# DeltaNet stage of a hybrid layer: scan, inverse, solve and pair preparation in a fixed program order on VectorE and ScalarE, with preparation in pieces two pairs ahead

## The chip, the cores and the metric

The kernel runs as one program on one core of a Trainium2 chip. The time is device time in microseconds, the median of several executions. Engines are named as in the profile: PE is TensorE's matmul, PEld its weight load, DVE is VectorE, ACT is ScalarE, POOL is GpSimd, SP is SyncE, which issues the DMA loads. Each engine takes its instructions in the order in which the program holds them.

## The reference

One layer over 512 latent tokens and 256 context tokens, width 1024, float32. Its token mixing joins softmax attention with a bidirectional gated DeltaNet of 8 heads of 128; the DeltaNet is the part that matters here:

```
# S_t = a_t (I - beta_t k_t k_t^T) S_{t-1} + beta_t k_t v_t^T,  o_t = S_t^T q_t, in chunks
gam = cumsum(log_a)                         # within the chunk
dec = exp(gam_c - gam_s) for c >= s, else 0
a_mat = strict_lower(beta * dec * (k k^T)) + I
u, w = triangular_solve(a_mat, [beta * v, beta * exp(gam) * k])
k_dec, g_last = k * exp(gam_last - gam), exp(gam_last)
q_dec, p = q * exp(gam), dec * (q k^T)
# scan over chunks: v' = u - w S;  o = q_dec S + p v';  S = g_last S + k_dec^T v'
```

It runs once in each direction, over the context first and then over the latent tokens. Chunks are 128 tokens in the kernel, so 6 of them to a head (2 of context, 4 latent).

## The kernel before

The layer is one long stream of projections (128x512 matmuls of split float32 operands, three for each product: high by high, low by high, high by low). The DeltaNet stage lies between 353 and 842 us of the span. Its 8 heads go in 4 pairs, p = 0 to 3, and each pair passes through five parts:

- `gdn_prep(p)` loads kT, and for each of the two heads (hh) and two directions (d) a broadcast of the cumulative decay `gamdr`, into NN and Gb (128x768). A mask is added (`NN<-NN,cst`, `Gb<-Gb,cst`), ACT takes six exponentials, and the two are summed (`NN<-NN,Gb`). It also makes the small tile g and its transpose gT.
- `gdn_solve` multiplies NN by the products k k^T (`pk`, on PE), lays the diagonal 32x32 blocks out as C, transposes to X, scales by gT, and inverts by a loop of 31 steps, each a `prod<-X,R` and an `R<-R,prod`. Then R is scaled by gT and transposed in 32x32 blocks into o_tr and o_nt. The loop is on DVE for pair 0 and on POOL for the others (SPOOL = '123').
- `gdn_inv(p)` builds the whole inverse (TTm) from the blocks, in four groups of products on PE that start with `pb<-o_tr,NN` and `pb<-o_nt,NN`.
- `gdn_scan(p)` runs six steps in both directions: `pb<-S,kT`, the residual r on DVE, `pb<-r,TTm`, then dk (ACT) and dl (DVE), the state S, the output oacc. Decay masks M2 (called M in the profile) come from `decay_mask`, one for each of four latent chunks; the last two steps add `pb<-dl,M` into oacc.
- `gdn_out(p)` normalises oacc, transposes it on PE, multiplies by the gate sz, and splits it into the high and low operands (g_s, g_n, g_k, g_m) of the last DeltaNet projection.

PE's order in this stage is pinned to the order of the program. Around the DeltaNet parts `weave` puts steps of `filler`, the layer's other projections, at set rates; a step of filler is three matmuls. `wait(n)` is n steps of filler alone: WK of them go before the first solve, W0 between the first solve and the first inverse, W1 after each scan. In the stage of pair p, `gdn_inv(p)` is interleaved with the solve of pair p+1, and then comes the scan of pair p beside the output of pair p-1. DVE's and ACT's order there is set by a scheduler, with priorities that the code gives (`early`, `sooner`, `solver`, `first`). Elementwise operations go through small helpers (`tt`, `ts`, `stt`, `act`), so most of DVE's and ACT's rows carry the lines of those: L108, L112 and L114, L117, L120.

Of the kernel before, what the change touches and what calls it, by code (L numbers as in the profile page):

```python
# [6 lines left out]
F32 = mybir.dt.float32  # L7
# [7 lines left out]
P = 128  # L15
D = 1024
# [14 lines left out]
POPS = (1, 3, 5, 7)  # L31
CHUNK, WK, W0, W1, RI, RS, RO = 1, 24, 66, 0, 3.0, 2.8, 2.0
RI0 = 2.4
# [45 lines left out]
def hybrid_layer_body(tc, x, ctxt, xT, consts, cols, rows, w_mod1, w_mod2, w_db, w_aq, w_cm, w_pa, w_pd, w_out,  # L79
# [23 lines left out]
    def dump(name, ap):  # L103
        if dbg is not None and name in dbg:
            SP.dma_start(dbg[name], ap)

    def tt(out, a, b, op, eng=None):
        (eng or V).tensor_tensor(out=out, in0=a, in1=b, op=op)  # L108

    def ts(out, a, s1, op0, s2=None, op1=None, eng=None):  # L110
        if op1 is None:
            (eng or V).tensor_scalar(out=out, in0=a, scalar1=s1, scalar2=None, op0=op0)  # L112
        else:
            (eng or V).tensor_scalar(out=out, in0=a, scalar1=s1, scalar2=s2, op0=op0, op1=op1)  # L114

    def stt(out, a, s, b, op0, op1):
        V.scalar_tensor_tensor(out=out, in0=a, scalar=s, in1=b, op0=op0, op1=op1)  # L117

    def act(out, a, f=AF.Copy, **kw):
        A.activation(out, a, f, **kw)  # L120

# [12 lines left out]
    with es:  # L134
# [738 lines left out]

        def gdn_prep(p, eng=G):
            kT = gq.tile([P, 2, NA], F32, name="kT", tag="kT", bufs=2)
            for hh in range(2):
                SP.dma_start(kT[:, hh, :], kTd[2 * p + hh])
            g = gq.tile([P, 32], F32, name="g", tag="g", bufs=2)
            gT = gq.tile([P, 32], F32, name="gT", tag="gT", bufs=2)
            V.memset(g[:, 24:32], 0.0)  # L880
# [6 lines left out]
            V.transpose(gT, g)  # L887
            NN = gq.tile([P, 12, P], F32, name="NN", tag="NN", bufs=2)
            for hh in range(2):
                u = slice(6 * hh, 6 * hh + 6)  # L890
                Gb = gq.tile([P, 6, P], F32, name="Gb", tag="Gb", bufs=1)
                for d, D in ((0, NN[:, u, :]), (1, Gb)):
                    r0 = d * 48 + p * 12 + hh * 6
                    SP.dma_start(D.rearrange("p a b -> p (a b)"),
                                 gamdr[r0:r0 + 6, :].rearrange("a b -> (a b)").partition_broadcast(P))
                    tt(D, D, msk_s[d].unsqueeze(1).to_broadcast([P, 6, P]), ALU.add, eng)
                    for c in range(6):
                        act(D[:, c, :], D[:, c, :], AF.Exp, scale=-1.0, bias=gam[:, r0 + c:r0 + c + 1])
                tt(NN[:, u, :], NN[:, u, :], Gb, ALU.add, eng)
            return [kT, gT, NN]  # L900

        def gdn_solve(pre, eng):
# [11 lines left out]
            with solver():  # L914
                q4 = lambda nm: gq.tile([P, 32, 32], F32, name=nm, tag="q4", bufs=3)
                C = q4("C")
                for b in range(4):
                    sb = slice(32 * b, 32 * b + 32)
                    V.transpose(C[sb, :, 12:24].rearrange("p j u -> p u j"), NN[sb, :, sb])
# [3 lines left out]
                V.transpose(flat(X), flat(C))  # L923
# [4 lines left out]
                if True:  # L928
                    for j in range(31):
                        m, n = 31 - j, j + 1  # L930
                        prod = gq.tile([P, 272], F32, name="prod", tag="prod")
                        pv = prod[:, 0:m * n].rearrange("p (i k) -> p i k", k=n)
                        tt(pv, X[:, j, j + 1:32].unsqueeze(2).to_broadcast([P, m, n]),
                           R[:, j:j + 1, 0:n].to_broadcast([P, m, n]), ALU.mult, eng)
                        tt(R[:, j + 1:32, 0:n], R[:, j + 1:32, 0:n], pv, ALU.add, eng)
                tt(R, R, gT.unsqueeze(2).to_broadcast([P, 32, 32]), ALU.mult)
                o_tr = q4("o_tr")
                V.transpose(o_tr.rearrange("p u s -> p s u"), R)
                o_nt = q4("o_nt")
                V.transpose(o_nt.rearrange("p u s -> p s u"), R.rearrange("p i k -> p k i"))  # L940
            pre += [o_tr, o_nt]

        def gdn_inv(p, pre):
# [13 lines left out]
            with sooner():  # L957
                for i, ((d, a, b), py) in enumerate(zip(AB, pys)):
                    (V.tensor_copy if i % 2 else act)(Y1[q(a)], py[q(a)])
# [9 lines left out]
            with sooner():  # L969
                for (d, e, f), pz in zip(AB, pzs):  # L970
                    (act if e % 2 else V.tensor_copy)(TTm[q(e), d, :, q(f)], pz[q(e)])
                for d in range(2):
                    a, b = TOP[d]
                    V.transpose(Tm[q(b), :, 32 * (a % 2):32 * (a % 2) + 32], TTm[q(a), d, :, q(b)])
            yield WY[1]

            for hh in range(2):
# [5 lines left out]
                with sooner():  # L983
                    for d in range(2):
                        sA, sB = HV[d]
                        (V.tensor_copy if d else act)(Y2[hh][sA], pys[d][sA])
                yield WY[2 + hh]
# [22 lines left out]

        def gdn_scan(p, pre, seqs):
            kT = pre[0]
# [25 lines left out]

            masks = {c: decay_mask(c) for c in (4, 3, 5, 2)}
            PTs = {}  # L1040
            for st in range(6):
                lat = st >= 2
                if st == 2:
                    oacc = gpool[0].tile([P, 2, 4, P], F32, name="oacc", tag="oacc")
# [24 lines left out]
                for d in range(2):  # L1069
# [7 lines left out]
                    if lat:  # L1077
                        dl = gpool[0].tile([P, 2, P], F32, name="dl", tag="dl", bufs=6)
                        V.tensor_copy(dl, pds[d][:, 0:2, :])
                        dls[(d, c)] = dl  # L1080
                    if st < 5:
# [70 lines left out]
        def gsplit(h):  # L1152
            if h % 2 == 0:
# [4 lines left out]
                elif h == 4:  # L1158
                    ts_ = [gq.tile([P, 12, P], F32R, name="g_n", tag="NN", bufs=2),
                           gq.tile([P, 2, NA], F32R, name="g_k", tag="kT", bufs=2)]  # L1160
                else:
                    ts_ = [gq.tile([P, 2, NA], F32R, name="g_k", tag="kT", bufs=2)]
                    ls = [gpool[0].tile([P, 2, 2, P], F32R, name="g_m", tag="M2", bufs=4) for _ in range(2)]
# [15 lines left out]
        def run(g):  # L1179
            for _ in g:  # L1180
                pass

        with early():
            pre = gdn_prep(0, V if P0 else G)
        pas_es, y_es, yt = ExitStack(), ExitStack(), []
# [116 lines left out]
        def stage(p, pre, nxt):  # L1302
            inv = gdn_inv(p, pre)
            if nxt is not None:
                yield from both(inv, gdn_solve(nxt, G if p + 1 in SPOOL else V))
            else:
                yield from inv

        for p in range(NP):
            cur = pre  # L1310
            pre = gdn_prep(p + 1) if p + 1 < NP else None
            g = stage(p, cur, pre)
# [3 lines left out]
            g = gdn_scan(p, cur, gdn_load(p))  # L1316
            out = (None, gdn_out(0), gdn_out(1), gdn_reload())[p]
# [266 lines left out]
```

## Time and profile before

| | |
|---|---|
| median of 3 runs | 1308.92 us (1308.15 to 1310.53) |
| profiled execution | 1304.85 us, its span 1303.1 us |
| PE busy | 1224.8 us, 94% of the span |
| PEld busy | 1024.0 us, 79% |
| DVE busy | 846.9 us, 65% |
| ACT busy | 625.9 us, 48% |
| POOL busy | 308.9 us, 24% |
| DMA | 170.82 MB, mean 131 GB/s |

A row of a timeline gives start, duration, engine, line, operation, and output <- inputs; a bracket at its end gives the time for which its engine had been idle, and what ended that. A row of PE's waits gives who was waited for, the total, how many times, and the longest. A row of a tile gives minimum, median and maximum duration in ns and the first and last start. In the table by stage each row gives the busy time of the engines in that stretch, then the granted TensorE clock (1.00 is full), the share of time in which the DMA engines were busy, and GB/s.

### The profile page before, as it was taken

Reading aid. Unit: us, or ns where it says so; the run is one execution under the profiler, and the core shown is the slowest. Engines: PE = TensorE matmul, PEld = TensorE weight load, DVE = VectorE, ACT = ScalarE, POOL = GpSimd, SP = SyncE. Lnnn points to the kernel's source line nnn. Section 1 sums busy time; section 2 is a strip of 40 time slices with the busy share of each in tenths; the row PEclk is TensorE's granted clock in tenths of the full one; section 3 lists DMA queues with packets and bytes.
Section 4 is the critical chain, followed back from the end, with each engine's and each line's share of the span. In section 5 each row is a group of like instructions: output and inputs, shape, how many; then the busy total and the mean of one; then the engine's idle time right before and its main releaser. Section 6 shows DMA issues by size and latency. Waiting matters only on the chain.

```text
span 1303.1 us, 20844 instructions
## 1 busy us (share of the span) xinstructions
PE 1224.8 (94%) x7835; PEld 1024.0 (79%) x7835; DVE 846.9 (65%) x1625; ACT 625.9 (48%) x1403; POOL 308.9 (24%) x364
## 2 busy tenths in 40 slices
PE   6899999999967999899998999999999999999997
PEld 3487878899856878778787888778988888888886
DVE  5886977777759986675665556555676666653223
ACT  5454656666576665474444443233454444442221
POOL 1753420000133249659546400000000000000000
PEclk9999999999989999999999999999999999999998
DMA  8656731121383342543632654374032323332331
GB/s 318 228 169 200 233 109 65 65 82 57 116 239 104 123 141 93 177 135 106 195 123 97 188 169 147 120 234 155 19 112 97 97 97 97 97 93 89 98 93 66
DMA packets 70790, 170.82 MB, mean 131 GB/s; under 512 B 7872, under 2 KB 18720, under 8 KB 69280
## 3 DMA queue, kind: packets, MB, share of 16 engines
q1 hardware_dynamic: 70688, 169.47, 39.4%
q8 instruction: 62, 1.02, 0.3%
q14 instruction: 40, 0.33, 0.1%
HBM read 144.23 MB, written 25.21 MB: 130 GB/s over the span
## 4 chain that ended last, share of the span: by engine, by line
PE 66%; POOL 11%; DVE 8%; DMA 5%; issue 3%; ACT 3%; SPq 0%; POOLq 0%; DVEq 0%; ACTq 0%
PE mc L87 32%; PE mb L87 17%; POOL R L108 4%; PE pq L87 4%; POOL prod L108 4%; PE pb L87 4%; PE pS L87 3%; PE ab L87 2%; PE ab L91 1%; DMA Gb<-gamdr 1%; DMA M<-gamdr 1%; PE xb L91 1%; DVE wlo L108 1%; PE pk L87 1%; DMA sz<-gdr 1%
## 5 line engine op out<-in xcount | busy, mean ns | idle before, releaser
L108 DVE TENSOR_TENSOR wlo<-wraw,whi 128x1024 fp32r<-128x1024 f32 x152 | 187.5, 1235 | 163.3 <-ACT whi L120 161.1
L120 ACT ACTIVATE whi<-wraw 128x1024 fp32r<-128x1024 f32 x152 | 159.0, 1048 | 207.3 <-PE mc L87 112.0
L87 PE MATMUL mb<-hxH,whi 128*128 128x512 f32 x384 | 163.6, 426 | 3.2 <-DVE R L108 3.0
L87 PE MATMUL mb<-hxL,whi 128*128 128x512 f32 x384 | 153.6, 400 | 0.0
L87 PE MATMUL mb<-hxH,wlo 128*128 128x512 f32 x384 | 153.2, 399 | 0.0
L87 PE MATMUL mc<-h2H,whi 128*128 128x512 f32 (+1 forms) x376 | 142.9, 380 | 0.3 <-ACT whi L120 0.3
L87 PE MATMUL mc<-h2H,wlo 128*128 128x512 f32 (+1 forms) x376 | 142.1, 378 | 0.5 <-DVE wlo L108 0.5
L87 PE MATMUL mc<-h2L,whi 128*128 128x512 f32 (+1 forms) x376 | 140.7, 374 | 0.0
L108 POOL TENSOR_TENSOR rc<-rc,mhalf 128x2 f32<-128x2 f32 x4 | 3.2, 812 | 461.2 <-DVE rc L114 461.2
L87 PEld LDWEIGHTS mb<-hxH,wlo 128*128 128x128 f32 x384 | 73.1, 190 | 18.0
L87 PEld LDWEIGHTS mb<-hxH,whi 128*128 128x128 f32 x384 | 73.9, 192 | 14.8 <-issue 3.2
L87 PEld LDWEIGHTS mc<-h2H,wlo 128*128 128x128 f32 x376 | 70.5, 188 | 15.3 <-DVE wlo L108 1.0
L87 PEld LDWEIGHTS mb<-hxL,whi 128*128 128x128 f32 x384 | 73.7, 192 | 10.1
L87 PEld LDWEIGHTS mc<-h2L,whi 128*128 128x128 f32 x376 | 70.6, 188 | 13.7
L87 PEld LDWEIGHTS mc<-h2H,whi 128*128 128x128 f32 x376 | 70.7, 188 | 12.7 <-ACT whi L120 0.5
L87 PE MATMUL mc<-aH,whi 128*128 128x512 f32 (+1 forms) x198 | 73.4, 371 | 0.6 <-DVE x L117 0.6
L87 PE MATMUL mc<-aH,wlo 128*128 128x512 f32 (+1 forms) x198 | 73.1, 369 | 0.0
L87 PE MATMUL mc<-aL,whi 128*128 128x512 f32 (+1 forms) x198 | 73.1, 369 | 0.0
L117 DVE SCALAR_TENSOR_TENSOR u<-mc,col,u 128x511 f32<-128x511 f32 x88 | 65.4, 747 | 1.4
L108 POOL TENSOR_TENSOR prod<-X,R 128x31 f32<-128x31 f32 (+15 forms) x93 | 53.5, 575 | 22.2 <-DVE X L108 15.3
L108 POOL TENSOR_TENSOR R<-R,prod 128x31 f32<-128x31 f32 (+15 forms) x93 | 57.1, 614 | 6.8
L87 PE MATMUL pq<-whi,hxH 128*128 128x256 f32 x192 | 55.8, 291 | 0.0
(354 smaller groups left out, 3069.8 us busy)
## 6 DMA issues: line engine op xcount, KB each, us to landing
wraw<-in_w_cm_dram SPq DMA_DIRECT2D x48, 512.0 KB, 3.9
wraw<-in_w_up_dram SPq DMA_DIRECT2D x44, 512.0 KB, 3.7
wmd<-in_w_mod_dram SPq DMA_DIRECT2D x64, 256.0 KB, 3.7
wm<-in_w_mod_dram SPq DMA_DIRECT2D x8, 1024.0 KB, 8.9
wraw<-in_w_down_dram SPq DMA_DIRECT2D x16, 512.0 KB, 3.6
wraw<-in_w_aq_dram SPq DMA_DIRECT2D x12, 512.0 KB, 4.9
M<-gamdr SPq DMA_DIRECT2D x64, 64.0 KB, 4.5
wraw<-in_w_pa_dram SPq DMA_DIRECT2D x8, 512.0 KB, 4.0
```

Of the source, the lines that this page charges most:

```text
L87: i = nc.tensor.matmul(*a, **k)
L91: i = nc.tensor.transpose(*a, **k)
L108: (eng or V).tensor_tensor(out=out, in0=a, in1=b, op=op)
L117: V.scalar_tensor_tensor(out=out, in0=a, scalar=s, in1=b, op0=op0, op1=op1)
L120: A.activation(out, a, f, **kw)
```

## The change

1. `kept(g)` runs a generator with a flag set; `ordered` then pins each DVE and ACT instruction that the generator emits behind the instruction that the program emitted last on that engine, filler included. Solve, preparation of pairs 1 to 3, inverse and scan run so. POOL is not pinned.
2. `gdn_prep` becomes a generator that gives way between its loads, each mask addition and the sum. Pair 1's runs among the steps of W0, and pair p+2's beside the scan of pair p. All mask additions and sums are now on DVE; before, those of pairs 1 to 3 were on POOL. Gb has two buffers instead of one, kT three instead of two.
3. The last product of the solve, R by gT, is on POOL for pairs 1 to 3.
4. o_tr and o_nt leave the end of the solve for `end()`. The scan of pair p calls it for pair p+1 in its last step, behind the copy of dl for d = 1. For pair 0 it is called after W0.
5. The decay masks are made one at each of the scan's first four steps, where all four came ahead of the scan.
6. WK goes from 24 to 30, W0 from 66 to 60, W1 from 0 to 2. The two steps of W1 put six filler matmuls between the end of a scan and the next inverse.

```
-CHUNK, WK, W0, W1, RI, RS, RO = 1, 24, 66, 0, 3.0, 2.8, 2.0
+CHUNK, WK, W0, W1, RI, RS, RO = 1, 30, 60, 2, 3.0, 2.8, 2.0
...
+    keep = [False]
+    def ordered(i, eng=None):
+        return tc.keep_in_program_order(i) if keep[0] and eng is not G else i
+    def kept(g):
+        while True:
+            keep[0] = True
+            try:
+                w = next(g)
+            except StopIteration:
+                return
+            finally:
+                keep[0] = False
+            yield w
...
-        (eng or V).tensor_tensor(out=out, in0=a, in1=b, op=op)
+        ordered((eng or V).tensor_tensor(out=out, in0=a, in1=b, op=op), eng)
...
-        def gdn_prep(p, eng=G):
-            kT = gq.tile([P, 2, NA], F32, name="kT", tag="kT", bufs=2)
+        def gdn_prep(p, pre):
+            kT = gq.tile([P, 2, NA], F32, name="kT", tag="kT", bufs=3)
...
+            for hh in range(2):
+                Gb = gq.tile([P, 6, P], F32, name="Gb", tag="Gb", bufs=2)
+                for d, D in ((0, NN[:, u, :]), (1, Gb)):
+                    SP.dma_start(...)
+                yield
+                for d, D in ((0, NN[:, u, :]), (1, Gb)):
+                    tt(D, D, msk_s[d].unsqueeze(1).to_broadcast([P, 6, P]), ALU.add)
+                    for c in range(6):
+                        act(D[:, c, :], D[:, c, :], AF.Exp, scale=-1.0, bias=gam[:, r0 + c:r0 + c + 1])
+                    yield
+                tt(NN[:, u, :], NN[:, u, :], Gb, ALU.add)
...
-                tt(R, R, gT.unsqueeze(2).to_broadcast([P, 32, 32]), ALU.mult)
-                o_tr = q4("o_tr")
-                V.transpose(o_tr.rearrange("p u s -> p s u"), R)
-                o_nt = q4("o_nt")
-                V.transpose(o_nt.rearrange("p u s -> p s u"), R.rearrange("p i k -> p k i"))
+                tt(R, R, gT.unsqueeze(2).to_broadcast([P, 32, 32]), ALU.mult, eng)
+            def end():
+                with solver():
+                    for nm, src in (("o_tr", R), ("o_nt", R.rearrange("p i k -> p k i"))):
+                        o = q4(nm)
+                        blocks(o.rearrange("p u s -> p s u"), src)
+                        pre.append(o)
...
-            masks = {c: decay_mask(c) for c in (4, 3, 5, 2)}
+                if st < 4:
+                    c = (4, 3, 5, 2)[st]
+                    masks[c] = decay_mask(c)
...
                     if st < 5:
...
+                    elif d == 1:
+                        end()
...
-        weave(gdn_solve(pre, G if 0 in SPOOL else V), RK)
-        weave(wait(W0), 1.0)
+        weave(kept(gdn_solve(pres[0], G if 0 in SPOOL else V)), RK)
+        weave(both(wait(W0), kept(gdn_prep(1, pres[1]))), 1.0)
+        gdn_end(pres[0])
         for p in range(NP):
+            g = kept(gdn_inv(p, pres[p]))
+            if p + 1 < NP:
+                g = both(g, kept(gdn_solve(pres[p + 1], G if p + 1 in SPOOL else V)))
             weave(g, RI if p else RI0)
...
+            g = kept(gdn_scan(p, pres[p], gdn_load(p), (lambda: gdn_end(pres[p + 1])) if p + 1 < NP else lambda: None))
+            if p + 2 < NP:
+                g = both(g, kept(gdn_prep(p + 2, pres[p + 2])))
```

On SP, before the first solve, the loads of pair 0's second Gb stood behind the masks M of its scan. Before:

```order
L1023 DMA M_5591<-gamdr 128x128 x4
L1023 DMA M_5602<-gamdr 128x128 x3
L197 DMA wraw<-in_w_cm_dram 128x1024
L1023 DMA M_5602<-gamdr 128x128
L1023 DMA M_5613<-gamdr 128x128 x3
L894 DMA Gb<-gamdr 128x768
```

Now, on SP, from the two loads of pair 0's kT on:

```order
L899 DMA kT<-kTd_105 128x768
L899 DMA kT<-kTd_106 128x768
L909 DMA NN<-gamdr 128x768
L909 DMA Gb<-gamdr 128x768
L909 DMA NN<-gamdr 128x768
L909 DMA Gb<-gamdr 128x768
```

Both Gb of pair 0 are loaded behind their NN; the masks and the token tiles of the scan come later in SP's order.

On DVE, in the last steps of pair 0's scan, the end of pair 1's solve (R, o_tr, o_nt) stood ahead of the last r. Before:

```order
L108 TENSOR_TENSOR R<-R,gT 128x1024
L108 TENSOR_TENSOR oacc<-oacc,pb 128x2x128 x2
L938 STREAM_TRANSPOSE o_tr<-R 128x32x32
L940 STREAM_TRANSPOSE o_nt<-R 128x32x32
L117 SCALAR_TENSOR_TENSOR r<-pb,eg,vtok 128x128 x2
L887 STREAM_TRANSPOSE gT<-g 128x32
L117 SCALAR_TENSOR_TENSOR r<-pb,eg,vtok 128x128 x2
L1079 COPY dl<-pb 128x256 x2
```

Now, on DVE at the same place (t is an eviction of the filler, Y the first evictions of inv(1)):

```order
L133 SCALAR_TENSOR_TENSOR r<-pb,eg,vtok 128x128 x4
L139 COPY dl<-pb 128x256
L124 TENSOR_TENSOR wlo<-wraw,whi 128x1024
L133 SCALAR_TENSOR_TENSOR oacc<-pb,eg,oacc 128x128 x2
L139 COPY dl<-pb 128x256
L142 STREAM_TRANSPOSE o_tr<-R 128x32x32
L142 STREAM_TRANSPOSE o_nt<-R 128x32x32
L133 SCALAR_TENSOR_TENSOR t_6107<-mb,col,t_6107 128x511
L133 SCALAR_TENSOR_TENSOR oacc<-pb,eg,oacc 128x128 x2
L124 TENSOR_TENSOR oacc<-oacc,pb 128x2x128
```

R by gT has gone to POOL, and both transposes stand between the last dl and the last additions to oacc.

On PE, at the end of the last scan, the last products with dl are followed by the last filler (atH, atL: attention projection; g_s, g_n, g_k, g_m: DeltaNet projection by head). Before:

```order
L87 MATMUL pb<-dl,M_8788 128x128 x4
L87 MATMUL pb<-dl,M_8799 128x128 x4
L87 MATMUL mb<-atH_8632,whi 128x512
L87 MATMUL mb<-atL_8633,whi 128x512
L87 MATMUL mb<-atH_8632,wlo 128x512
L87 MATMUL mb<-g_s,whi 128x512 x2
```

Now, on PE at the same place:

```order
L87 MATMUL mb<-g_s,whi 128x512
L87 MATMUL mb<-g_n,whi 128x512
L87 MATMUL mb<-g_s,wlo 128x512
L87 MATMUL pb<-dl,M_9013 128x128 x4
L87 MATMUL pb<-dl,M_9128 128x128 x4
L87 MATMUL mb<-g_s,whi 128x512
```

The filler runs 18 matmuls further ahead of the last scan than before: from the last products with dl to the end of this pair of output projections 33 filler matmuls follow, where 51 did.

More of the change, by code (lines that the diff above doesn't have):

```diff
@@ L105, in dump, with copy, blocks @@
             SP.dma_start(dbg[name], ap)
+    keep = [False]
[11 more added lines that the diff above has]
+            yield w
     def tt(out, a, b, op, eng=None):
[L108 removed]
+        ordered((eng or V).tensor_tensor(out=out, in0=a, in1=b, op=op), eng)
     def ts(out, a, s1, op0, s2=None, op1=None, eng=None):
         if op1 is None:
[L112 removed]
+            ordered((eng or V).tensor_scalar(out=out, in0=a, scalar1=s1, scalar2=None, op0=op0), eng)
         else:
[L114 removed]
+            ordered((eng or V).tensor_scalar(out=out, in0=a, scalar1=s1, scalar2=s2, op0=op0, op1=op1), eng)
     def stt(out, a, s, b, op0, op1):
[L117 removed]
+        ordered(V.scalar_tensor_tensor(out=out, in0=a, scalar=s, in1=b, op0=op0, op1=op1))
     def act(out, a, f=AF.Copy, **kw):
[L120 removed]
+        ordered(A.activation(out, a, f, **kw))
+    def copy(out, a):
+        ordered(V.tensor_copy(out, a))
+    def blocks(out, a):
+        ordered(V.transpose(out, a))
     def split(hi, lo, src):
@@ L879, in gdn_prep @@
             gT = gq.tile([P, 32], F32, name="gT", tag="gT", bufs=2)
-            V.memset(g[:, 24:32], 0.0)
+            NN = gq.tile([P, 12, P], F32, name="NN", tag="NN", bufs=2)
+            pre += [kT, gT, NN]
+            for hh in range(2):
+                u = slice(6 * hh, 6 * hh + 6)
+                Gb = gq.tile([P, 6, P], F32, name="Gb", tag="Gb", bufs=2)
+                for d, D in ((0, NN[:, u, :]), (1, Gb)):
+                    r0 = d * 48 + p * 12 + hh * 6
+                    SP.dma_start(D.rearrange("p a b -> p (a b)"),
+                                 gamdr[r0:r0 + 6, :].rearrange("a b -> (a b)").partition_broadcast(P))
+                yield
+                for d, D in ((0, NN[:, u, :]), (1, Gb)):
+                    r0 = d * 48 + p * 12 + hh * 6
+                    tt(D, D, msk_s[d].unsqueeze(1).to_broadcast([P, 6, P]), ALU.add)
[3 more added lines that the diff above has]
+                tt(NN[:, u, :], NN[:, u, :], Gb, ALU.add)
+            ordered(V.memset(g[:, 24:32], 0.0))
             for d in range(2):
@@ L886, in gdn_prep @@
                     tt(g[:, u], g[:, u], rkk[2 * p + hh], ALU.mult)
[L887 to L900, printed above, removed]
+            blocks(gT, g)
         def gdn_solve(pre, eng):
@@ L927, in gdn_solve, with gdn_end @@
                 G.memset(flat(R)[:, 0:1024:33], 1.0)
[L928 to L935, printed above, removed]
-                tt(R, R, gT.unsqueeze(2).to_broadcast([P, 32, 32]), ALU.mult)
-                o_tr = q4("o_tr")
-                V.transpose(o_tr.rearrange("p u s -> p s u"), R)
-                o_nt = q4("o_nt")
-                V.transpose(o_nt.rearrange("p u s -> p s u"), R.rearrange("p i k -> p k i"))
-            pre += [o_tr, o_nt]
+                for j in range(31):
+                    m, n = 31 - j, j + 1
+                    prod = gq.tile([P, 272], F32, name="prod", tag="prod")
+                    pv = prod[:, 0:m * n].rearrange("p (i k) -> p i k", k=n)
+                    tt(pv, X[:, j, j + 1:32].unsqueeze(2).to_broadcast([P, m, n]),
+                       R[:, j:j + 1, 0:n].to_broadcast([P, m, n]), ALU.mult, eng)
+                    tt(R[:, j + 1:32, 0:n], R[:, j + 1:32, 0:n], pv, ALU.add, eng)
+                tt(R, R, gT.unsqueeze(2).to_broadcast([P, 32, 32]), ALU.mult, eng)
[5 more added lines that the diff above has]
+                        pre.append(o)
+            pre.append(end)
+        def gdn_end(pre):
+            pre.pop()()
         def gdn_inv(p, pre):
@@ L958, in gdn_inv @@
                 for i, ((d, a, b), py) in enumerate(zip(AB, pys)):
-                    (V.tensor_copy if i % 2 else act)(Y1[q(a)], py[q(a)])
+                    (copy if i % 2 else act)(Y1[q(a)], py[q(a)])
                 for d, b in ((0, 2), (0, 3), (1, 0), (1, 1), (0, 0), (0, 1), (1, 2), (1, 3)):
@@ L970, in gdn_inv @@
                 for (d, e, f), pz in zip(AB, pzs):
-                    (act if e % 2 else V.tensor_copy)(TTm[q(e), d, :, q(f)], pz[q(e)])
+                    (act if e % 2 else copy)(TTm[q(e), d, :, q(f)], pz[q(e)])
                 for d in range(2):
                     a, b = TOP[d]
-                    V.transpose(Tm[q(b), :, 32 * (a % 2):32 * (a % 2) + 32], TTm[q(a), d, :, q(b)])
+                    blocks(Tm[q(b), :, 32 * (a % 2):32 * (a % 2) + 32], TTm[q(a), d, :, q(b)])
             yield WY[1]
@@ L985, in gdn_inv @@
                         sA, sB = HV[d]
-                        (V.tensor_copy if d else act)(Y2[hh][sA], pys[d][sA])
+                        (copy if d else act)(Y2[hh][sA], pys[d][sA])
                 yield WY[2 + hh]
@@ L1009, in gdn_load, with gdn_scan @@
             return qT, ktok, vtok
-        def gdn_scan(p, pre, seqs):
+        def gdn_scan(p, pre, seqs, end):
             kT = pre[0]
@@ L1037, in intra @@
                 return M2
-            masks = {c: decay_mask(c) for c in (4, 3, 5, 2)}
-            PTs = {}
+            masks, PTs = {}, {}
             for st in range(6):
                 lat = st >= 2
+                if st < 4:
+                    c = (4, 3, 5, 2)[st]
+                    masks[c] = decay_mask(c)
                 if st == 2:
@@ L1078, in gdn_scan @@
                         dl = gpool[0].tile([P, 2, P], F32, name="dl", tag="dl", bufs=6)
-                        V.tensor_copy(dl, pds[d][:, 0:2, :])
+                        copy(dl, pds[d][:, 0:2, :])
                         dls[(d, c)] = dl
@@ L1159, in gsplit @@
                     ts_ = [gq.tile([P, 12, P], F32R, name="g_n", tag="NN", bufs=2),
-                           gq.tile([P, 2, NA], F32R, name="g_k", tag="kT", bufs=2)]
+                           gq.tile([P, 2, NA], F32R, name="g_k", tag="kT", bufs=3)]
                 else:
-                    ts_ = [gq.tile([P, 2, NA], F32R, name="g_k", tag="kT", bufs=2)]
+                    ts_ = [gq.tile([P, 2, NA], F32R, name="g_k", tag="kT", bufs=3)]
                     ls = [gpool[0].tile([P, 2, 2, P], F32R, name="g_m", tag="M2", bufs=4) for _ in range(2)]
@@ L1181, in run @@
                 pass
+        pres = [[] for _ in range(NP + 1)]
         with early():
-            pre = gdn_prep(0, V if P0 else G)
+            run(gdn_prep(0, pres[0]))
         pas_es, y_es, yt = ExitStack(), ExitStack(), []
```

14 lines of the change are left out of this document (2 added, 12 removed).

## The prediction

> **What bounds the kernel now.** I read the page's slices first, then PE's waits in the DeltaNet stretch (353 to 842 us), then busy time by stage, then the rows around the longest waits. On the page:
>
> ```profile
> PE   6899999999967999899998999999999999999997
> DVE  5886977777759986675665556555676666653223
> PEclk9999999999989999999999999999999999999998
> ```
>
> PE is full nearly everywhere; the one dip lies in slices 12 and 13 (358 to 423 us), where DVE is full. A gain can only come from PE's idle time and from the clock that drops after it. PE's waits between 360 and 850 us (total, times, longest):
>
> ```profile
> PE pb L87 <- DVE r L117: 13.0, 7, 4.2
> PE pk L87 <- DVE NN L108: 8.6, 1, 8.6
> PE xb L91 <- DVE co L117: 6.4, 3, 2.9
> PE mb L87 <- DVE R L108: 3.0, 1, 3.0
> PE pb L87 <- DVE oacc L117: 2.9, 2, 2.8
> ```
>
> That is 33.9 us, all of it for DVE. By stage (us; busy PE, PEld, DVE, ACT, POOL with instructions; granted clock, DMA share, GB/s):
>
> ```profile
> 380.00:400.00 20.00, 10.54 (x57) 8.86 (x55) 13.14 (x16) 13.64 (x33) 8.36 (x8) 0.74 0.32 83
> 400.00:420.00 20.00, 15.79 (x85) 13.23 (x86) 19.49 (x38) 11.11 (x35) 7.67 (x4) 1.00 0.45 152
> 451.00:546.00 95.00, 88.09 (x749) 73.27 (x748) 70.72 (x131) 52.01 (x139) 66.39 (x95) 0.98 0.42 137
> 546.00:642.00 96.00, 89.37 (x806) 75.65 (x806) 64.46 (x130) 50.23 (x140) 60.98 (x88) 1.00 0.43 139
> 642.00:738.00 96.00, 90.29 (x747) 76.78 (x732) 56.10 (x117) 44.51 (x104) 49.88 (x79) 0.95 0.42 138
> ```
>
> From 400 to 420 us DVE is the bound (19.5 of 20 us); in the three stages with a solve beside the scan PE is, with gaps that DVE's order makes.
>
> **A. The first solve, up to inv(0).** Rows of SP, DVE, PE and POOL; in brackets the idle time before:
>
> ```profile
> 375.61 0.38 SPq L894 DMA_DIRECT2D Gb<-gamdr  x1
> 381.02 0.40 PE L87 MATMUL mb<-hxH,wlo 128*128 128x512 f32 x1
> 387.38 0.96 DVE L108 TENSOR_TENSOR NN<-NN,Gb 128x768 f32<-128x768 f32 x1 [4.46 <-ACT Gb L120]
> 390.01 1.22 PE L87 MATMUL pk<-kT 128*128 128x128 f32 x4 [8.59 <-DVE NN L108]
> 397.43 2.29 POOL L108 TENSOR_TENSOR NN<-NN,Gb 128x768 f32<-128x768 f32 x1 [2.79 <-ACT Gb L120]
> 398.13 1.63 DVE L108 TENSOR_TENSOR prod<-X,R 128x31 f32<-128x31 f32 x1
> 399.80 0.21 DVE L108 TENSOR_TENSOR R<-R,prod 128x31 f32<-128x31 f32 x1
> ```
>
> The second Gb of pair 0 is issued at 375.61, behind the M2 masks and in a single buffer; DMA, mask add, six exponentials and the sum end at 388.3, and PE stands 8.59 us. With two buffers it is loaded directly behind pair 0's other three, ahead of the masks, so this wait goes. But WK puts six more filler steps ahead of pk: 18 matmuls. Their spacing is in these rows:
>
> ```profile
> 824.33 0.39 PE L87 MATMUL mb<-atL,whi 128*128 128x512 f32 x1
> 824.56 0.40 PE L87 MATMUL mb<-atH,wlo 128*128 128x512 f32 x1
> ```
>
> 18 × 0.233 = 4.2 us, so pk moves from 390.0 to about 381.4 + 4.2 = 385.6 and the chain behind it gains 4.4 us. W0 is six steps shorter, so PE has the same work up to inv(0), and DVE decides. The loop of pair 0 runs on DVE, and four of its operations lie beside POOL's adds for pair 1: `prod` at 398.13 takes 1.63 us beside the add at 397.43, where its neighbour takes 0.21. The four stretched ones are 1.4, 1.5, 1.2 and 1.7 us too long (longest against median in the group below), 5.9 us together.
>
> ```profile
> L108 DVE TENSOR_TENSOR R<-R,prod x31: 192/368/2051, 399.8 to 445.8; 128x31 f32<-128x31 f32 x2, 128x60 f32<-128x60 f32 x2, 128x87 f32<-128x87 f32 x2, 128x112 f32<-128x112 f32 x2
> L108 POOL TENSOR_TENSOR NN<-NN,Gb 128x768 f32<-128x768 f32 x6 | 11.6, 1928 | 4.8 <-ACT Gb L120 4.8
> L108 DVE TENSOR_TENSOR NN<-NN,Gb x2: 945/952/959, 368.7 to 387.4; 128x768 f32<-128x768 f32 x2
> L940 DVE STREAM_TRANSPOSE o_nt<-R x4: 1928/1948/2140, 449.2 to 713.0; 128x1024 f32<-128x1024 f32 x4
> ```
>
> The 18 adds of pairs 1 to 3 leave POOL (1.93 us each in this group) for DVE (0.95 each, six to a pair, 5.7 us). Two of pair 1's I expect ahead of o_tr, +1.9 us in a stretch where DVE is full. Pair 0's o_nt ended at 451.1; it should end 4.4 + 5.9 − 1.9 = 8.4 us sooner, and with the shorter priority detours of the pinned order I take **9 us** (5 if all six adds come before the transposes, 13 if DVE also stops holding up PE's filler at `mb<-DVE R` and `xb<-DVE co`). The slow clock of 380 to 400 us (0.74) goes too, worth nothing while DVE decides.
>
> [...]
>
> **B. The three stages.** R*gT, o_tr and o_nt of the next pair (rows of DVE, then the PE wait behind them):
>
> ```profile
> 530.62 1.23 DVE L108 TENSOR_TENSOR R<-R,gT 128x1024 f32<-128x1024 f32 x1 [2.58 <-POOL R L108]
> 532.43 1.91 DVE L938 STREAM_TRANSPOSE o_tr<-R 128x1024 f32<-128x1024 f32 x1
> 534.21 1.93 DVE L940 STREAM_TRANSPOSE o_nt<-R 128x1024 f32<-128x1024 f32 x1
> 536.39 1.82 PE L87 MATMUL pb<-r,TTm 128*128 128x128 f32 x8 [4.16 <-DVE r L117]
> 538.24 0.42 DVE L1079 COPY dl<-pb 128x256 f32<-128x256 f32 x1 [0.61 <-PE pb L87]
> 629.99 1.16 PE L87 MATMUL pb<-dl,M 128*128 128x128 f32 x8 [2.76 <-DVE oacc L117]
> 586.97 1.98 DVE L117 SCALAR_TENSOR_TENSOR co<-co,t 128x512 f32<-128x512 f32 x1 [2.98 <-ACT co L120]
> 629.34 0.60 DVE L117 SCALAR_TENSOR_TENSOR oacc<-pb,eg,oacc 128x128 f32<-128x128 f32 x2
> 711.48 0.77 PE L87 MATMUL pb<-r,TTm 128*128 128x128 f32 x2 [2.50 <-DVE r L117]
> 715.20 1.65 PE L87 MATMUL pb<-r,TTm 128*128 128x128 f32 x6 [2.95 <-DVE r L117]
> ```
>
> DVE, in order, waits up to 4.1 us for POOL's R and then works 5 us, while the scan's r or oacc stands behind: 4.16, 2.76 and 5.45 us of PE. The change takes R*gT to POOL and o_tr, o_nt behind the last dl copy, so these waits go.
>
> What is late next: inv(p+1) stands directly behind. After that dl copy DVE has o_tr 1.91, o_nt 1.93, two oacc steps (0.6), at times a weight split (128x1024, as R*gT with its 1.23), then an oacc addition (128x256, about as dl's 0.42) that free a bank for inv: 4.9 to 6.1 us. The dl copy itself now comes about 1 us after PE's last S,qT products (an oacc step and a copy stand between). PE has meanwhile 6 to 9 filler matmuls, 1.16 us of dl products and the six matmuls of W1: 4.0 to 4.7 us. So a new wait of 1.2 to 3.1 us per boundary (4.9 + 1 − 4.7, 6.1 + 1 − 4.0); I take 1.9, nearer the end without a split, since a split stands there at one boundary of three in the order.
>
> The adds of pairs 2 and 3 (5.7 us of DVE in stages 0 and 1 at 74 and 67% load) can each hold a scan step for under 1 us; 1 us a stage. Pair 1's and 2's solve chain on POOL loses the adds between its operations, which nobody waited for once the transposes are late anyway. R*gT on POOL costs an estimated 1.93 × 1024/768 = 2.6 us against DVE's 1.23, on nothing's path if R is there when DVE reaches o_tr.
>
> M2's adds and loads, now one chunk a step, are still two steps (over 20 us) ahead of their use; kT with three buffers only loads sooner. Both 0, hidden by the scan; if that cover failed, a late mask would stop PE as the late Gb did, for up to 8.6 us.
>
> - Stage 0: 4.2 − 1.9 − 1 + 1 (clock 0.98 to 1.00 over half the stage) = **2.3**.
> - Stage 1: 2.8 + 1.9 (waits behind DVE work that POOL's adds stretch, such as co at 586.97, 1.98 us) − 1.9 − 1 = **1.8**.
> - Stage 2: 5.5 + 3.5 (0.05 × 96 = 4.8 us of clock at most) − 1.9 = **7.1**; no preparation is left in it.
>
> **C. The end.** Rows of PE and DVE:
>
> ```profile
> 822.32 1.95 PE L87 MATMUL pb<-dl,M 128*128 128x128 f32 x16
> 830.52 1.66 DVE L112 TENSOR_SCALAR oacc<-oacc,f 128x128 f32<-128x128 f32 x8
> 837.03 0.75 DVE L117 SCALAR_TENSOR_TENSOR sz<-pb,gwh,sz 128x512 f32<-128x512 f32 x1 [2.74 <-DMA sz<-szd]
> 838.50 0.50 PE L87 MATMUL mb<-g_k,whi 128*128 128x512 f32 x1 [2.47 <-ACT g_k L120]
> ```
>
> gdn_out(3) is a chain of 14.2 us from the last dl product (824.3) to 838.50, which PE bridges with filler and still waits 2.47. W1 spends eight steps earlier; 18 of those 24 matmuls come from ahead of this wait (33 instead of 51 follow the last dl product), 4.2 us less cover. PE's wait grows to some 7 us, in three pieces close together. After 2.5 and 2.95 us in a row at 711 to 715 the clock fell; its mean over stage 2 was 0.95. I add 1.3: **−5.5 us**.
>
> [...]
>
> **Sum.** 9 + 2.3 + 1.8 + 7.1 − 5.5 = 14.7 us off the profiled execution's 1304.85 (span 1303.1). The median of the runs shown is 4 us above it, and I carry the difference: 1308.9 − 14.7 = **1294**. Ends: A 5 to 13, the stages 4 to 18, the end −8 to −3 give gains of 1 to 28, not all at once; 8 in 10 is 1281 to 1309.
>
> **Rivals.**
>
> 1. *Slower: R is late at o_tr.* DVE would stop in order at o_tr with the scan's last oacc steps and all filler evictions behind. Pair 3 waited for R until 709.18, 67 us after its inversion began at 642; with R*gT on POOL 70 us. Pair 1 waited until 530.6, 79 us after 451.1, some 12 of them POOL's six adds (6 × 1.93). The last dl copy comes 87 us after the start (538.2), some 84 in the new kernel. Margin 10 us or more. It decides if POOL's chain takes over 10 us longer than I think plus 4.9 us (14.7 / 3) at each boundary: DVE's moved adds would have to hold up POOL as POOL's held up DVE, more than twice their own length (six of 0.95 us a pair). At 6.5 us late each the three boundaries lose 20 and the time is 1314. Against it: pair 3's chain ran at 67 us with all of DVE's splits beside it.
> 2. *No change: DVE becomes the bound.* 17 us more DVE work, and 5 us of transposes between dl and inv, uncovered: if boundaries cost 4.5 instead of 1.9 (−8), the adds 2 a stage (−2) and A gives 5, it is 14.7 − 14 = 1, 1308. For it: 19.5 of 20 us at 400 to 420.
> 3. *The clock and the filler's waits give more.* PE's waits for `mb<-DVE R`, `xb<-DVE co` (9.4 us in all) go with the pinned order, A gives 13, boundaries are covered by W1: 14.7 + 4 + 5 = 24, 1285. For it: these waits lie where POOL's adds slow DVE. Against: the first, at 372, is earlier than anything changed.
>
> [...]
>
> **Chances.** My forecast 0.5; rival 3 0.2; rival 2 0.17; rival 1 0.13. No change means within 0.2% (2.6 us), about what a measurement of this kernel can tell. Rival 2 splits into 0.08 same, 0.05 still faster and 0.04 slower; of my forecast 0.02 falls below that bound. Faster 0.73, same 0.10, slower 0.17. Where the sign is positive its own range is 1284 to 1303.
>
> **What would show it.** A: pk without a wait, `prod` of pair 0 all near 0.2 to 0.4 us, inv(0) 9 us sooner. B: no r behind o_tr; a wait of about 2 us at the first products of each inv(1) to inv(3), by o_nt or oacc; clock 1.00 in stage 2. C: 7 us of waits before the last g_k. Wrong, if DVE shows idle time for POOL's R ahead of o_tr, if inv(0) starts less than 5 us sooner, or if stage 2 keeps a wait above 4 us.

## The result: 1357 us, 3.6% slower, and the profile after

The changed kernel takes 1356.97 us (median of 4 runs, 1353.72 to 1357.79) against 1308.54 us: ratio 1.036, 95% interval 1.034 to 1.038. The forecast was 1294. The experiments below were timed in other sessions, each beside the kernel before, whose median moved between 1306.7 and 1308.5 us; so their ratios compare better than their medians do. The profiled execution has a span of 1355.7 us, 52.6 more than before. First the slices of the page after:

```profile
PE   7899999999898677897999997989999999999997
DVE  6887977777679765576464654555576666553233
PEclk9999999999999787899999998989999999999999
```

PE's dip of slices 12 and 13 is gone, and a longer one stands in slices 14 to 17 (440 to 576 us), with a lower clock: the stage of pair 0. By stage, from one inverse's start to the next (busy PE, PEld, DVE, ACT, POOL; granted clock, DMA share, GB/s); the first row is the stretch up to inv(0), the last the stage of pair 3 with the end:

```profile
353.00:446.00 93.00, 78.25 (x433) 65.50 (x432) 72.85 (x148) 52.23 (x141) 16.20 (x16) 0.95 0.55 190
446.00:574.00 128.00, 99.79 (x752) 83.71 (x752) 76.22 (x151) 57.29 (x156) 56.09 (x86) 0.85 0.32 102
574.00:682.00 108.00, 96.36 (x775) 80.88 (x773) 70.73 (x149) 54.37 (x149) 57.44 (x86) 0.95 0.37 118
682.00:777.00 95.00, 90.11 (x820) 76.23 (x823) 56.60 (x120) 43.26 (x104) 53.63 (x86) 1.00 0.43 137
777.00:891.00 114.00, 98.53 (x729) 80.62 (x717) 56.70 (x132) 41.84 (x111) 8.87 (x10) 0.94 0.40 127
```

Against 95, 95, 96 and 102 us before, stage 0 is 33 us longer, stage 1 13, stage 2 no longer, stage 3 12. Stage 0 also opens at a low clock (0.50 from 446 to 451 us), behind the wait for o_tr in the list below; without these 5 us its mean is 0.86. Part of the loss is PE's own work at a lower clock (0.85, before 0.98 from 451 to 546 us): with 752 matmuls against 749, PE is busy 99.8 us in stage 0, where it was 88.1. PE's waits of 340 to 920 us:

```profile
PE pb L87 <- DVE r L133: 25.9, 7, 7.2
PE pb L87 <- ACT dk L136: 10.1, 9, 1.8
PE pb L87 <- DVE o_tr L142: 8.1, 1, 8.1
PE pk L87 <- DVE NN L124: 5.1, 3, 2.3
PE pb L87 <- DVE S L133: 3.9, 1, 3.9
```

The wait for r was to go, and it has doubled (13.0 before). What DVE does ahead of r stands in its rows, here with those of POOL and PE around the longest wait:

```profile
491.31 0.40 DVE L130 TENSOR_SCALAR rkq<-gkss 128x4 f32<-128x4 f32 x1 [1.62 <-ACT xb L136]
494.34 0.56 POOL L124 TENSOR_TENSOR prod<-X,R 128x220 f32<-128x220 f32 x1
494.86 1.02 POOL L124 TENSOR_TENSOR rkq<-rkq,mhalf 128x4 f32<-128x4 f32 x1
495.92 0.58 DVE L128 TENSOR_SCALAR rkq<-rkq 128x4 f32<-128x4 f32 x1 [4.20 <-POOL rkq L124]
496.41 1.11 DVE L133 SCALAR_TENSOR_TENSOR r<-pb,eg,vtok 128x128 f32<-128x128 f32 x4
496.81 2.07 PE L87 MATMUL pb<-r,TTm 128*128 128x128 f32 x8 [7.23 <-DVE r L133]
```

`rkq` is not the DeltaNet stage's at all: it is the query norm in the filler's head projection, a chain over four engines. PE transposes into `xb`, ACT sums squares, DVE adds epsilon (`rkq<-gkss`), POOL takes the power, DVE scales. Each of its two DVE steps can wait: the first for ACT, the second for POOL, whose queue holds the solve's loop. The scan's r is pinned behind them and waits too. In the kernel before, DVE's rows of the same place are in this order:

```profile
486.68 1.11 DVE L117 SCALAR_TENSOR_TENSOR r<-pb,eg,vtok 128x128 f32<-128x128 f32 x4
492.16 0.19 DVE L114 TENSOR_SCALAR rkq<-gkss 128x4 f32<-128x4 f32 x1 [4.37 <-ACT xb L120]
494.61 0.52 DVE L112 TENSOR_SCALAR rkq<-rkq 128x4 f32<-128x4 f32 x1 [1.24 <-POOL rkq L108]
```

The same waits, 4.37 and 1.24 us, but r had gone first and nobody stood behind. The two other long waits of stage 0 are of the same kind (rows of DVE, POOL and PE of the changed kernel):

```profile
527.01 0.17 DVE L130 TENSOR_SCALAR rkq<-gkss 128x4 f32<-128x4 f32 x1 [3.97 <-ACT xb L136]
528.61 1.87 DVE L128 TENSOR_SCALAR rkq<-rkq 128x4 f32<-128x4 f32 x1 [1.43 <-POOL rkq L124]
530.88 2.05 PE L87 MATMUL pb<-r,TTm 128*128 128x128 f32 x8 [4.81 <-DVE r L133]
...
557.73 0.17 DVE L130 TENSOR_SCALAR rkq<-gkss 128x4 f32<-128x4 f32 x1 [3.21 <-ACT xb L136]
559.22 0.72 POOL L124 TENSOR_TENSOR M<-M,cst 128x256 f32<-128x256 f32 x1 [28.75 <-DMA M<-gamdr]
561.24 1.02 POOL L124 TENSOR_TENSOR rkq<-rkq,mhalf 128x4 f32<-128x4 f32 x1
562.29 0.17 DVE L128 TENSOR_SCALAR rkq<-rkq 128x4 f32<-128x4 f32 x1 [4.39 <-POOL rkq L124]
562.77 2.08 PE L87 MATMUL pb<-r,TTm 128*128 128x128 f32 x8 [5.27 <-DVE r L133]
```

At 559 POOL had stood still for 28.75 us, until the DMA of a decay mask; behind this addition stood rkq's power, behind that DVE's scaling, behind that r, behind that PE. Over the whole stretch DVE waited 17.6 us for POOL's rkq (6.9 before) and 14.2 us for ACT ahead of rkq (9.6 before). In stage 3 another filler chain does it, the gating and split of the reloaded sz:

```profile
816.67 0.75 DVE L133 SCALAR_TENSOR_TENSOR sz<-pb,gwh,sz 128x512 f32<-128x512 f32 x1 [3.89 <-DMA sz<-szd]
819.22 1.12 PE L87 MATMUL pb<-r,TTm 128*128 128x128 f32 x6 [4.16 <-DVE r L133]
831.52 0.69 DVE L124 TENSOR_TENSOR g_n<-sz,g_s 128x512 fp32r<-128x512 f32 x1 [3.92 <-ACT g_s L136]
832.53 1.36 PE L87 MATMUL pb<-r,TTm 128*128 128x128 f32 x8 [2.73 <-DVE r L133]
```

### The profile page after: what moved, and what is told of

It reads as the page before. It is cut to its first block, busy times and chain, and to the rows that moved or that the text cites. A ratio compares the mean times of both kernels' runs of the same rounds, so it can differ in the third digit from the quotient of the medians.

```text
span 1355.7 us, 20825 instructions
## 1 busy us (share of the span) xinstructions
PE 1247.8 (92%) x7835; PEld 1041.0 (77%) x7835; DVE 854.8 (63%) x1640; ACT 626.3 (46%) x1403; POOL 281.5 (21%) x349
## 4 chain that ended last, share of the span: by engine, by line
PE 50%; POOL 5%; DVE 4%; ACT 3%; DMA 2%; issue 2%; SPq 0%; POOLq 0%; DVEq 0%; ACTq 0%
PE mc L87 31%; PE mb L87 13%; PE pb L87 5%; POOL prod L124 2%; POOL R L124 2%; DMA M<-gamdr 1%; ACT whi L136 1%; DVE wlo L124 1%; PE pk L87 1%; DMA sz<-szd 0%; ACT C L136 0%; PE pqk L87 0%; POOL rkq L124 0%; ACT TTm L136 0%; ACT xb L136 0%
## 5 line engine op out<-in xcount | busy, mean ns | idle before, releaser
L87 PE MATMUL mb<-hxH,whi 128*128 128x512 f32 x384 | 167.2, 435 | 0.2 <-DVE t L133 0.2
L87 PE MATMUL mb<-hxL,whi 128*128 128x512 f32 x384 | 156.6, 408 | 0.0
L87 PE MATMUL mb<-hxH,wlo 128*128 128x512 f32 x384 | 156.0, 406 | 0.0
```

The lines of the kernel that those rows point to most:

```text
L87: i = nc.tensor.matmul(*a, **k)
```

## The experiments

Theory: the pins cost the time, because they put scan steps behind filler instructions that wait for other engines, the query norm above all. Rivals: the additions moved to DVE (A); o_tr and o_nt late, masks by step, or W1 (B); pins as such, whatever stands ahead (C).

| kernel | median us | ratio to before (95%) |
|---|---|---|
| changed kernel | 1356.97 | 1.036 (1.034 to 1.038) |
| pins alone, on the kernel before | 1356.13 | 1.037 (1.036 to 1.039) |
| changed, no pins | 1313.91 | 1.005 (1.003 to 1.007) |
| changed, preparation's additions on POOL | 1351.06 | 1.033 (1.030 to 1.036) |
| changed, query norm emitted late | 1334.12 | 1.020 (1.019 to 1.022) |
| changed, query norm on POOL | 1322.74 | 1.011 (1.007 to 1.014) |
| the same, last scan unpinned | 1311.53 | 1.003 (1.002 to 1.004) |
| changed, scans unpinned | 1320.19 | 1.010 (1.007 to 1.013) |
| changed, ACT unpinned | 1351.60 | 1.034 (1.030 to 1.037) |
| changed, only o_tr and o_nt pinned | 1298.65 | 0.993 (0.991 to 0.996) |
| the same, query norm on POOL | 1297.57 | 0.992 (0.991 to 0.993) |
| only o_tr, o_nt pinned; W0 66, W1 0 | 1302.91 | 0.995 (0.994 to 0.997) |
| the same, query norm on POOL | 1301.07 | 0.995 (0.993 to 0.996) |

**Pins alone.** On the kernel before, inverse and scan run through `kept`, with `copy` and `blocks` in them:

```
-            inv = gdn_inv(p, pre)
+            inv = kept(gdn_inv(p, pre))
-            g = gdn_scan(p, cur, gdn_load(p))
+            g = kept(gdn_scan(p, cur, gdn_load(p)))
```

> The kernel before, with only the scan's and the inverse's DVE and ACT instructions pinned in program order; nothing else changed. Theory: the pins alone put r behind rkq, so 15 to 35 us slower than before, 1325 to 1345. Rivals A and B: within 5 us of before, 1304 to 1314.

It was worse than the upper bound, 1356.1 us: as slow as the whole change. PE's longest waits there, and the rows around the longest:

```profile
PE pb L87 <- DVE r L133: 26.6, 8, 7.2
PE pb L87 <- ACT dk L136: 18.0, 11, 5.6
495.33 0.53 DVE L130 TENSOR_SCALAR rkq<-gkss 128x4 f32<-128x4 f32 x1 [5.22 <-ACT xb L136]
497.32 0.55 DVE L128 TENSOR_SCALAR rkq<-rkq 128x4 f32<-128x4 f32 x1 [1.46 <-POOL rkq L124]
498.18 2.08 PE L87 MATMUL pb<-r,TTm 128*128 128x128 f32 x8 [7.16 <-DVE r L133]
```

The r wait is the changed kernel's (25.9, 7, 7.2), behind the same two steps, with neither late transposes, nor additions moved, nor W1. Rivals A and B are out as the main cause. Other waits are not the same: those for dk are longer here (18.0 against 10.1), so the equal times are in part chance, and what dk costs was not tested on this kernel.

**No pins.**

```
-        return tc.keep_in_program_order(i) if keep[0] and eng is not G else i
+        return i
```

> The changed kernel with no instruction of DVE or ACT pinned; everything else of the change stays (pieces of preparation, additions on DVE, R by gT on POOL, late o_tr and o_nt, masks by step, WK, W0, W1). Theory (pinned scan steps stand on DVE behind the filler's query norm, which waits for ACT and for POOL's queue): the r waits of 4.8 to 7.2 us go, 1290 to 1305 us. Rival A (the additions on DVE slow the scan): still 1340 or more. Rival B (late o_tr, masks or W1 cost the time): still 1330 or more.

1313.9 us, 43 us better than the changed kernel and 9 above the top of what I had expected. Without pins the scheduler moves o_tr and o_nt back to where DVE waits for POOL's R, ahead of the scan's steps (a row of DVE's waits, then one of PE):

```profile
DVE o_tr L142 <- POOL R L124: 7.9, 3, 3.2
722.25 2.08 PE L87 MATMUL pb<-r,TTm 128*128 128x128 f32 x8 [6.61 <-DVE r L133]
```

**Additions on POOL.**

```
-                    tt(D, D, msk_s[d]..., ALU.add)
+                    tt(D, D, msk_s[d]..., ALU.add, G if p else V)
-                tt(NN[:, u, :], NN[:, u, :], Gb, ALU.add)
+                tt(NN[:, u, :], NN[:, u, :], Gb, ALU.add, G if p else V)
```

> The changed kernel, with the mask additions and sums of pairs 1 to 3 back on POOL. Theory: the r waits stay or grow (POOL's queue is longer, and rkq's power stands in it), 1350 to 1370 us. Rival A (additions on DVE slow the scan): 1320 to 1335.

1351.1 us. Rival A falls: moving the additions back is worth 6 us of the 48 at most by the medians and 5 by the ratios, whose intervals overlap.

**Query norm late, and on POOL.** First the sums went straight into rkq and the rest of the norm into gdn_out:

```
+            if part == 0:
+                kss = rkq[h]
...
             for hh in range(2):
+                rsqrt(rqh(p, hh), rqh(p, hh), 1.0, 4 * EPS)
+                ts(rqh(p, hh), rqh(p, hh), 128.0 ** -0.5, ALU.mult)
```

> The changed kernel, pins kept, but the query norm is taken out of the filler: the sums of squares go straight into rkq, and the two small DVE steps and POOL's power run in gdn_out, where rkq is first needed. Theory: DVE no longer waits for rkq ahead of r (17.6 us for POOL, 14.2 for ACT in the changed kernel), PE's r waits of 7.2, 4.8, 5.3 and the S wait of 3.9 shrink below 2 and the clock of stages 0 and 1 recovers: about 1357 - 21 - 12 = 1324 us. Rival A (additions on DVE) and rival C (the pinned order as a whole, with weight splits and evictions ahead of the scan): 1345 to 1357.

1334.1 us, 23 less, and 10 short of the theory. Its trace gives a reason: gdn_out is not pinned, the scheduler put these steps back near their old place, and DVE still waited 15.7 us for POOL's rkq. So the second version took them off DVE, with the scale folded in, and pinned their first use:

```
+                    if part == 0:
+                        ts(rkq[h], kss[:, 0:n], 128.0, ALU.mult, 512 * EPS, ALU.add, G)
+                        tt(rkq[h], rkq[h], mhalf[:, 0:n], ALU.pow, G)
```

> The changed kernel, pins kept, with the query norm wholly on POOL (sum plus epsilon, scaled, and the power, two small POOL steps a head), so that no DVE instruction of it stands ahead of a scan step; its first use, in gdn_out, is pinned where the program has it. In the run before this one (norm late) the scheduler had put these DVE steps back to their old places, so 15.7 us of DVE waits for POOL were left. Theory 1 (the query norm on DVE is the larger part of the pins' price): 1315 to 1325 us, no r wait above 2 us in stage 0. Rival (any filler instruction ahead of a pinned step costs alike, the norm only the visible one): 1330 to 1340.

1322.7 us, 34 less than the changed kernel: two thirds of its loss hung on two small DVE steps a head. No r wait above 0.2 us is left in its stage 0 (446 to 549 us, 103 long instead of 128). Rival C's number, 1330 to 1340, was missed; but that other filler costs as well, where it waits, shows in the next run.

**The last scan unpinned as well.**

```
-            g = kept(gdn_scan(...))
+            g = gdn_scan(...)
+            g = kept(g) if p < 3 else g
```

> The changed kernel with the query norm on POOL (1322.7 us), and the last scan unpinned. Theory: in the last scan r waits 4.1 and 2.4 us behind the split of the reloaded sz, which waits for ACT and a DMA; unpinned these go with the slow clock after them, 1310 to 1317. Rival (these waits do not set the end): 1319 to 1325.

1311.5 us, 11 less. Both r waits of the last scan (4.1 and 2.4 us) are gone, and the clock of its stage is 0.99 (746 to 847 us), where the changed kernel has 0.94 in the table by stage. The edit frees the whole last scan, so that it is the split of sz alone is read from the rows and not isolated. Norm and last scan together make 45 of the 48 us.

**Scans unpinned, ACT unpinned.** One drops `kept` around every gdn_scan, the other `ordered` in `act`.

> The changed kernel with the four scans unpinned; solve, preparation of pairs 1 to 3 and inverse stay pinned. Theory (the price of the pins is paid in the scan, by r, S and dk behind filler): within 8 us of the unpinned kernel's 1314, so 1308 to 1322. Rival (pinned solve and inverse pay too, by NN, C, X and Y behind filler): 1330 to 1345.

> The changed kernel with ACT unpinned and DVE pinned. Theory (DVE's order is what costs, ACT's only the 10 us of PE waits for dk, some of which come from r being late): 1340 to 1357. Rival (ACT's order shares the price evenly): 1325 to 1338.

1320.2 us without pins in the scans, inside the range; 1351.6 us without ACT's. So the price is paid in the scan (37 us) and on DVE; freeing ACT is worth 5 us by the medians, 3 by the ratios, whose intervals overlap.

**Only o_tr and o_nt pinned.** This is the one part of the order that had a reason in the profile before:

```
-        ordered(V.transpose(out, a))
+        i = V.transpose(out, a)
+        if pin:
+            tc.keep_in_program_order(i)
...
+                        blocks(o.rearrange("p u s -> p s u"), src, keep[0])
```

> The changed kernel with only o_tr and o_nt of pairs 1 to 3 pinned (behind the last dl copy); all else on DVE and ACT is left to the scheduler. In the unpinned kernel these two went back ahead of the scan's steps, where PE lost 3.8, 2.9 and 6.6 us at three places. Theory: those waits go, a wait of 1 to 2 us per boundary comes, so 1314 - 13 + 5 = 1306 us, 1300 to 1310. Rival (the price moves to the boundary): 1311 to 1318.

1298.7 us, faster than the kernel before by 0.7% and 58 us faster than the change as it was made. Against the kernel without pins, these two pinned transposes are worth 15 us. By stage:

```profile
353.00:448.00 95.00, 79.71 (x432) 67.05 (x430) 79.29 (x179) 64.43 (x184) 16.55 (x16) 0.95 0.57 191
448.00:545.00 97.00, 90.29 (x750) 76.09 (x751) 68.85 (x131) 50.58 (x132) 54.67 (x85) 0.94 0.38 123
545.00:638.00 93.00, 90.28 (x773) 76.09 (x772) 65.05 (x136) 50.90 (x137) 57.30 (x88) 1.00 0.43 140
638.00:728.00 90.00, 88.66 (x763) 75.49 (x762) 58.05 (x118) 44.05 (x104) 54.37 (x85) 1.00 0.44 145
728.00:832.00 104.00, 97.33 (x773) 79.48 (x772) 56.63 (x132) 38.67 (x104) 8.89 (x10) 0.97 0.42 141
```

**With the norm on POOL, and with the old W1.** Three runs on that base; the norm as above, and `WK, W0, W1 = 30, 66, 0`:

> Only o_tr and o_nt of pairs 1 to 3 pinned, as in the run that beat the kernel before (1298.7 us), and the query norm wholly on POOL. Theory: unpinned, the scheduler had put rkq where little waited for it; what is left of it (7.3 us of DVE waits for POOL, 5.7 for ACT) costs PE at most the 3.0 us wait for the filler's t: 1294 to 1299. Rival (rkq's steps on POOL delay the solve chain there by more): 1300 to 1305.

> The same base (o_tr, o_nt pinned alone), with W0 back at 66 and W1 back at 0: six filler steps more ahead of inv(0), none between a scan and the next inverse. Theory: the wait of 5.3 us for o_tr at inv(0) is filled (6 x 0.7 = 4.2 us), each of three boundaries loses up to 1.4 us, and only two filler steps instead of eight are missing at the end, worth 4 us there: 1292 to 1298. Rival (boundaries lose all that they had): 1299 to 1304.

> All three together: o_tr and o_nt pinned alone, query norm on POOL, W0 66 and W1 0. Theory: gains add, 1289 to 1296. Rival: they share the same idle time, 1296 to 1300.

1297.6, 1302.9 and 1301.1 us: the first in its range, the second in its rival's, the third above both of its own. Unpinned, the norm is worth nothing that can be told from noise: the scheduler had set it where little waited. W0 at 66 and W1 at 0 cost 2.5 us by the ratios in the first pair, which was timed in two sessions (its intervals overlap), and 3.5 us in the second (its intervals don't meet); I had expected a gain of up to 7. Two boundaries have no cover then (rows of PE in the second run, W1 0):

```profile
544.65 0.24 PE L87 MATMUL pb<-o_tr,NN 32*32 32x32 f32 x2 [3.12 <-DVE oacc L124]
728.78 0.31 PE L87 MATMUL pb<-o_tr,NN 32*32 32x32 f32 x2 [3.21 <-DVE oacc L124]
```

With W1 at 2 the longest wait at a boundary of that base is 0.95 us. The lowest median is 1297.6 us, within noise of 1298.7.

## Why the prediction was wrong

**The step that failed: the pins have no price in it.** The sum went through additions, transposes, R by gT, masks and W1; of the first item of the change it says only "the shorter priority detours of the pinned order", as a gain in A, and rival 3 lets waits "go with the pinned order". The pins alone cost 49 us (1307.0 to 1356.1 in their session), more than three times the gain forecast. The work that the change adds a wait to is the scan's r, and what is queued ahead of it on DVE was not asked for beyond weight splits and o_tr. Both halves of the answer were to be had beforehand. DVE's order of the changed kernel has the two rkq steps directly ahead of the last r of scan 0 (one row before the piece shown above). And the trace of before has the price of what they wait for:

```profile
DVE rkq L114 <- ACT xb L120: 9.6, 5, 4.4
DVE rkq L112 <- POOL rkq L108: 6.9, 5, 3.0
```

The wait of 4.4 us had nothing behind it that PE needed: between 481 and 532 us PE has no wait above 0.49 us there. The change put r behind this chain, and PE waited 7.23 us. I had listed PE's waits alone and left DVE's idle time out, as if it were free; it was, in that order only.

**The rivals.** Rival 1 had the right sign and the right kind (DVE stopping in order for POOL's queue) with the wrong instruction: o_tr never waited for R in the changed kernel. That its price, up to 6.5 us at each of three places, is near the 7.2, 4.8 and 5.3 us found at r in stage 0 alone is chance. The chance of slower, 0.17, was too low for a change that fixes the order of two engines against work that was not costed.

**A, the first solve: 9 us forecast, 3 to 4 found.** Pair 0's `pk` no longer waits for NN, and POOL's additions no longer stretch the loop, as said (before, the four steps of the loop beside them took 1.60 to 2.05 us; now no step is above 0.94):

```profile
L124 DVE TENSOR_TENSOR prod<-X,R x31: 177/371/935, 396.2 to 440.7; 128x31 f32<-128x31 f32 x2, 128x60 f32<-128x60 f32 x2, 128x87 f32<-128x87 f32 x2, 128x112 f32<-128x112 f32 x2
444.25 1.92 DVE L142 STREAM_TRANSPOSE o_tr<-R 128x1024 f32<-128x1024 f32 x1
446.23 0.31 PE L87 MATMUL pb<-o_tr,NN 32*32 32x32 f32 x2 [8.07 <-DVE o_tr L142]
448.01 0.25 PE L87 MATMUL pb<-o_nt,NN 32*32 32x32 f32 x1 [1.47 <-DVE o_nt L142]
```

The longest prod is 0.94 us instead of 1.84. But the loop begins only 1.9 us sooner (396.2 against 398.1; I had 4.4), and from its first prod to its last R it lasts 45.0 us against 47.7, so 2.7 less, not 5.9. The 5.9 was too large: it measured the stretched operations against the median of all shapes, and the loop's own busy time fell by only 3.3 us (26.8 to 23.5). The two mask additions ahead of o_tr came as said (442.5 and 443.4). inv(0) gets going at 448.0 instead of 451.6, after 9.5 us of waits. The sign set for this, a start less than 5 us sooner, came true.

**B, the stages.** In the kernel with only o_tr and o_nt pinned the terms can be read without the pins' loss. Stage 2 is 6 us shorter (7.1 forecast) with the clock at 1.00 as said; stage 1 is 2 us shorter (1.8); stage 0 is 2.6 us longer, from 448.6 to 545.7, where 2.3 shorter was forecast. The r waits behind o_tr are gone there. But PE waits 5.3 and 1.5 us for o_tr and o_nt at inv(0), and the clock behind that is 0.50 from 448 to 453 us and 0.67 from 453 to 458, where the kernel before had 1.00; over the stage it is 0.94 instead of 0.98, and PE's busy time is 90.3 us instead of 88.1. The sum had a clock gain of 1 us there and no price for the slow clock behind the wait at inv(0). R by gT took 1.9 us on POOL, where 2.6 were estimated. The boundary wait, 1.9 forecast, adds up to 1.5 us at most in the changed kernel (0.74 and 0.74 at inv(1)); the longest single one is 1.2.

**C, the end.** 5.5 us were forecast, 1.2 found: in that kernel inv(3) starts 8.3 us sooner than before (728.9 against 737.1) and the span is 7.1 shorter. PE's waits in the last chain came in pieces, 0.8, 1.8 and 1.7 us, 4.3 where 7 were forecast, and the clock is 0.87 in the last 14 us and 0.97 over the stage, where it was 1.00 in both.

The four terms without pins were forecast as 14.7 us; the kernel that has them, with no pin but o_tr and o_nt, gained 8.0 us in the median of its session (1306.7 to 1298.7), 7.1 in span.

## What to carry to other kernels

Pinning DVE's order here turned waits of the instructions ahead into waits of those behind (4.20 us of DVE for rkq ahead of r, 7.23 us of PE for r); so before anything is pinned, list for the engine which instructions wait for another engine, small ones first, and see what the new order puts behind them. Idle time on an engine off the critical path was free only in the order in which it was measured: behind DVE's 4.37 and 1.24 us for rkq PE's next wait for r was 0.22 us. Pin the few instructions for which the profile shows a reason (here two transposes, worth 15 us against no pins), and leave the rest to the scheduler.

## What the runs showed of the hardware

The power of 128x4 elements took 1.02 us on POOL (494.86 us in the changed kernel), longer than the 128x220 product of the solve's loop ahead of it (0.56 us). And slow clock was a loss of its own: with waits of 7.2, 4.8 and 5.3 us in stage 0, and 8.1 at its start, the mean granted clock was 0.85 (before 0.98), and PE was busy 11.7 us longer (99.8 against 88.1) on nearly the same matmuls. I had put 1 to 3.5 us a stage to the clock.

In the kernel with only o_tr and o_nt pinned, a single wait of 2.99 us was followed by a clock of 0.50 (a row of PE, then one by stretch):

```profile
486.59 0.50 PE L87 MATMUL mb<-hxH,whi 128*128 128x512 f32 x1 [2.99 <-DVE t L133]
488.00:490.00 2.00, 2.00 (x8) 1.71 (x8) 0.66 (x2) 0.65 (x2) 1.76 (x4) 0.50 0.51 104
```

From 492 us on it was 1.00 again. In the kernel before, a wait of 3.02 us was followed by a clock of 1.00 (the same two kinds of row):

```profile
402.15 0.47 PE L87 MATMUL mb<-hxH,whi 128*128 128x512 f32 x1 [3.02 <-DVE R L108]
402.00:404.00 2.00, 1.85 (x9) 1.56 (x10) 1.83 (x7) 0.00 (x0) 0.83 (x1) 1.00 0.13 44
```

And in the changed kernel the clock was 0.56 from 470 to 472 us, behind a wait of 2.29 us at 468.73. So in these runs the length of a wait alone does not tell the clock behind it.
